# Down-projection of the last block: loads of weights and residual issued in turn with the activation blocks

## The chip, the cores and the metric

The kernel runs as one program on one core of a Trainium2 chip. The metric is device time in microseconds (us) of one execution. The time before is the median of three timed executions; one further execution was profiled, and every row shown here comes from that one.

## What is computed

The reference is a stack of two blocks on a sequence of 1024 tokens with 1024 features, in float32: a first block (attention with a pooled branch, then a gated convolution), and a second block (attention with a forgetting gate beside a short convolution, then a feed-forward part). The change lies in the very last part, the second half of the feed-forward part:

```python
hn = rms_norm_2(h, norm_mlp_g[layer])
a = jnp.square(jax.nn.relu(jnp.einsum('bld,df->blf', hn, w_ff1[layer])))
h = h + jnp.einsum('blf,fd->bld', a, w_ff2[layer])
h = rms_norm_2(h, final_norm_g)
```

The second product multiplies 1024 x 4096 activations by a 4096 x 1024 weight matrix, adds the residual and is followed by the final norm.

## The kernel before

**Precision and tiles.** Every float32 operand is split into a high and a low half of a shorter float type: `hi` (line 381) copies the high half on ScalarE (ACT), `lo` (line 384) takes the rest on VectorE (DVE). A product is then three matmuls (high by high, high by low, low by high), each 128 x 128 stationary by 128 x 512 moving.

**Seven steps instead of eight.** The product is done in the manner of Strassen and Winograd: the activations, the weights and the result are cut in two by two quarters, and seven products of quarters, the entries of `steps` (line 1720), replace eight. I number them 0 to 6 here. For a step the left operand is a stored combination of activation quarters (`11`, `s1`, `s2`, `s4`, `s3`, `12`, `22`), which the up-projection before (class `Up`, line 174) wrote to DRAM; the right operand is a combination of weight quarters, named `b11`, `t1`, `t2`, `b22`, `t3`, `b21`, `t4` after its function (lines 1678 to 1701).

**Inside a step** (loop at line 1733) the 2048 rows of the inner dimension are walked in eight blocks p of 256. Each block loads a tile `act` of 512 KB (line 1735, two buffers of the tag `wf`), splits it into `ah` and `al`, makes the right operand and splits it into `bh` and `bl` (three buffers each for the a and the b halves), and issues 24 matmuls: 4 banks of PSUM, 2 halves of 128 rows, 3 products. A step has 8 x 24 = 192 matmuls. After it, four additions on DVE (line 1763) put the banks onto the residual tile `res`.

**Where the right operands come from.** All of them call `weights` (line 1668), which loads a 512 KB tile of the weight matrix.
- Step 0 (`b11`) loads the eight tiles `x` and keeps them.
- Step 1 (`t1`) loads eight tiles `w` and subtracts `x` from them, into `x`, on DVE (line 1675).
- Step 2 (`t2`) loads eight tiles `y`, keeps them and forms `x` minus `y`. Step 3 (`b22`) uses `y` and loads no weights.
- Steps 4, 5 and 6 (`t3`, `b21`, `t4`) load eight tiles `w` each. Tiles `w` have two buffers (the tag `wh`).

**The residual** is loaded in four quarters of four DMAs of 256 KB (lines 1740 to 1743). They are written in the code behind block 3 of steps 0, 1, 2 and 4, ahead of the addition that needs them.

**What sets the order of the work.** The code is only traced in the order it is written. When the program is built, a scheduler that simulates the kernel in time gives each engine its own list of instructions: of those ready, each engine takes the one that is ready first, so an instruction that waits for nothing can come far ahead of its place in the code. The lists are fixed from then on: an engine runs its list in order, and an instruction that waits holds up all behind it. All loads of this part are in the list of SyncE's queue (SP), and those of the up-projection, its stores among them, too. Waiting for a buffer is such a wait: `act` of block p + 2 can be issued when `al` of block p has been made, because that was the last reader of the buffer.

Of the kernel before, what the change touches and what calls it, by code (L numbers as in the profile page):

```python
# [39 lines left out]
HALF = slice(0, 512), slice(512, 1024)  # L40
# [291 lines left out]
class Kernel:  # L332
# [1318 lines left out]
    def feed_down(self, one):  # L1651


        nc, a = self.nc, self.a
        hold = self.pool("d1", "right", 3)
        left = self.pool("d2", "left", 3)
        xp = self.psum_pool("pxdown", "pd")
        res_pool = self.pool("res3", "right")
        res = res_pool[1].tile([128, NT, D], F32, name="res")
        gfin = one.tile([128, D], F32, tag="last", name="gfin")  # L1660
        nc.sync.dma_start(out=gfin, in_=a["fing"].partition_broadcast(128))
        kept = {}

        def tile(name, p):
            pool = hold if p < 2 and name == "x" else left
            return pool[1].tile([128, 2, 512], F32, tag=f"{name}{p}", name=f"{name}{p}", bufs=1)

        def weights(j, l, p, t=None):
            t = t or self.stream.tile([128, 2, 512], F32, tag="wh", name="w2")
            r0 = 2048 * j + 256 * p  # L1670
            nc.sync.dma_start(out=t, in_=a["ff2"][r0:r0 + 256, HALF[l]].rearrange("(k p) c -> p k c", p=128))
            return t

        def minus(out, x, y):
            nc.vector.tensor_tensor(out=out, in0=x, in1=y, op=ALU.subtract)
            return out

        def b11(p):
            kept["x", p] = weights(0, 0, p, tile("x", p))
            return kept["x", p]  # L1680

        def t1(p):
            x = kept["x", p]
            return minus(x, weights(0, 1, p), x)

        def t2(p):
            kept["y", p] = weights(1, 1, p, tile("y", p))
            return minus(kept["x", p], kept["y", p], kept["x", p])

        def b22(p):  # L1690
            return kept["y", p]

        def t3(p):
            t = weights(0, 1, p)
            return minus(t, kept["y", p], t)

        def b21(p):
            return weights(1, 0, p)

        def t4(p):  # L1700
            return minus(kept["x", p], weights(1, 0, p), kept["x", p])

        def split(pool, tag, src):
            h, l = (pool[1].tile([128, 2, 512], F32R, tag=tag + x, name=tag + x) for x in "hl")
            self.hi(h, src)
            self.lo(l, src, h)
            return h, l

        def matmuls(bank, i, k, left, right, first, last, fresh):
            (ah, al), (bh, bl) = left, right  # L1710
            c = slice(i * 128, i * 128 + 128)
            for j, (st, mv) in enumerate(((ah, bh), (ah, bl), (al, bh))):
                nc.tensor.matmul(  # L1713
                    out=bank, lhsT=st[:, k, c], rhs=mv[:, k, :], start=(fresh and first and j == 0),
                    stop=(last and j == 2), skip_group_check=not fresh,
                )

        odd = None
        even = None
        steps = (  # L1720
            ("11", b11, 0, 0), ("s1", t1, 4, 1), ("s2", t2, 0, 1), ("s4", b22, 0, 1),
            ("s3", t3, 4, 1), ("12", b21, 0, 0), ("22", t4, 4, 0),
        )
        quarters = {0: (0, 0), 1: (4, 1), 2: (0, 1), 4: (4, 0)}
        for n, (name, right, t0, h) in enumerate(steps):
            fresh = n in (0, 1, 5)
            if n == 0:
                even = [self.bank("pd", 4) for _ in range(4)]
            elif fresh:
                odd = [self.pj(), self.pj(), self.ps(), self.ps()]  # L1730
            banks = odd if n % 2 else even
            ops = []
            for p in range(8):
                t = self.stream.tile([128, 2, 512], F32, tag="wf", name="act")
                nc.sync.dma_start(out=t, in_=self.act[name, p])
                ops.append((split(left, "a", t), split(hold, "b", right(p))))
                end = n == 6 and p >= 6
                if end and p == 6:
                    continue
                if p == 3 and n in quarters:  # L1740
                    r0, c = quarters[n]
                    for i in range(r0, r0 + 4):
                        nc.sync.dma_start(out=res[:, i, HALF[c]], in_=self.x3[i * 128:(i + 1) * 128, HALF[c]])
                if not end:
                    for k in range(2):
                        for i in range(4):
                            matmuls(banks[i], i, k, *ops[p], p + k == 0, p == 7 and k == 1, fresh)
            squares = {}
            if n == 6:
                for i in range(4):  # L1750
                    ms = squares[i] = self.tiny(2, "fms")
                    junk = left[1].tile([128, 512], F32, tag="r", name="junk")
                    self.half_square(ms, 1, res[:, t0 + i, HALF[1]], junk)
                    nc.gpsimd.tensor_scalar(
                        out=ms[:, 1:2], in0=ms[:, 1:2], scalar1=EPS_B, scalar2=None, op0=ALU.add
                    )
            for i in range(4):
                if n == 6:
                    for p in (6, 7):
                        for k in range(2):  # L1760
                            matmuls(banks[i], i, k, *ops[p], False, p == 7 and k == 1, fresh)
                x = res[:, t0 + i, HALF[h]]
                nc.vector.tensor_tensor(out=x, in0=x, in1=banks[i], op=ALU.add)
                if n > 4:
                    self.final_norm(t0 + i, [res[:, t0 + i, z] for z in HALF], gfin, left[1], squares.get(i))
        self.close(res_pool, hold, left, xp)
# [94 lines left out]
```

## Time and profile before

| | before |
|---|---|
| median of 3 runs | 1979.45 us (1978.23 to 1982.49) |
| profiled execution | 1975.94 us |
| span in its profile | 1974.2 us |
| TensorE (PE) busy | 1906.5 us, 97% |
| VectorE (DVE) busy | 1340.4 us, 68% |
| ScalarE (ACT) busy | 906.0 us, 46% |
| GpSimd (POOL) busy | 542.5 us, 27% |
| data moved by DMA | 212.15 MB, 107 GB/s on average |

The span is the time from the first to the last instruction in the profile; the profiled execution's own time is 1.7 us longer. Busy shares are means over the whole kernel; the part that the change touches is the stretch from about 1640 us to the end. A row of a timeline gives start, duration, engine, line, operation, output and inputs, and in brackets how long the engine had been idle before it and what ended that wait. A row with "x2" stands for two instructions in a row.

### The profile page before, as it was taken

The page shows a single profiled execution, that of the slowest core. Times are in us where ns is not written, and L with a number is a line of the kernel's source. Part 1 is how long each engine was busy: PE and PEld are TensorE (multiplying, and loading weights), DVE is VectorE, ACT ScalarE, POOL GpSimd, SP SyncE. Part 2 cuts the span into 40 slices and gives each one's busy share as a digit, 9 for nine tenths or more (in the row PEclk, how much of TensorE's full clock was granted, in tenths as well). Part 3 has the DMA queues.
Part 4 walks back from the last instruction along what each step waited for, and adds up shares of the span by engine and source line. Part 5 has one row for each costly group of instructions (what it writes and reads, how often), then busy time and mean ns, then how long its engine had stood idle before and what let it go on. Part 6 is the DMA issues. An engine that isn't in the chain of part 4 may idle for free. (4 is left out here: it accounts for less than half of the span.)

```text
span 1974.2 us, 25561 instructions
## 1 busy us (share of the span) xinstructions
PE 1906.5 (97%) x9584; PEld 1616.1 (82%) x9584; DVE 1340.4 (68%) x2045; ACT 906.0 (46%) x1577; POOL 542.5 (27%) x433
## 2 busy tenths in 40 slices
PE   7999999899999899999999999999999998999998
PEld 5888788687778678898999998887888886788886
DVE  7788656699898665565656655657776766754666
ACT  5556234456664665555444544324333323333333
POOL 4022602479997221001010101202433320000003
PEclk9999999999999999999999999999999999999999
DMA  4110143111122732111111202523534448622564
GB/s 151 51 47 26 67 135 117 40 54 52 36 79 85 236 107 73 45 44 44 48 49 44 76 27 99 192 98 102 171 133 166 149 160 321 228 96 96 192 214 149
DMA packets 122747, 212.15 MB, mean 107 GB/s; under 512 B 9576, under 2 KB 59112, under 8 KB 122624
## 3 DMA queue, kind: packets, MB, share of 16 engines
q1 hardware_dynamic: 120320, 206.34, 30.9%
q10 hardware_dynamic: 2304, 4.20, 0.6%
q8 instruction: 75, 1.23, 0.3%
q14 instruction: 48, 0.39, 0.1%
HBM read 156.46 MB, written 54.03 MB: 107 GB/s over the span
## 5 line engine op out<-in xcount | busy, mean ns | idle before, releaser
L1155 POOL TENSOR_TENSOR side<-side,tap 128x1024 f32<-128x1024 f32 (+1 forms) x99 | 235.6, 2386 | 24.9 <-ACT tap L1154 17.8
L1161 DVE SCALAR_TENSOR_TENSOR acc<-glu,dw,acc 128x1024 f32<-128x1024 f32 (+1 forms) x162 | 193.8, 1238 | 11.5 <-ACT acc L1159 10.2
L425 PE MATMUL pj<-c0h,wl 128*128 128x512 f32 (+1 forms) x496 | 187.8, 379 | 5.7 <-DVE wl L386 5.7
L425 PE MATMUL pj<-c0h,wh 128*128 128x512 f32 (+1 forms) x496 | 188.9, 381 | 4.3 <-ACT gt L1192 2.7
L425 PE MATMUL pj<-c0l,wh 128*128 128x512 f32 (+1 forms) x496 | 187.4, 378 | 0.0
L425 PE MATMUL pj<-c1h,wh 128*128 128x512 f32 (+1 forms) x496 | 176.3, 356 | 3.6 <-ACT sg L1129 1.8
L425 PE MATMUL pj<-c1l,wh 128*128 128x512 f32 (+1 forms) x496 | 177.0, 357 | 0.0
L425 PE MATMUL pj<-c1h,wl 128*128 128x512 f32 (+1 forms) x496 | 176.6, 356 | 0.0
L1154 ACT ACTIVATE tap<-glu,dw 128x1024 f32<-128x1024 f32 (+1 forms) x99 | 103.8, 1055 | 78.9 <-POOL side L1155 78.4
L386 DVE TENSOR_TENSOR al<-act,ah 128x1024 fp32r<-128x1024 f32 x56 | 68.3, 1223 | 91.5 <-ACT ah L382 91.3
L382 ACT ACTIVATE ah<-act 128x1024 fp32r<-128x1024 f32 x56 | 59.3, 1060 | 154.5 <-PE ps L1713 75.4
L382 ACT ACTIVATE ph<-pt 128x512 fp32r<-128x512 f32 (+3 forms) x144 | 72.8, 516 | 104.7 <-PE pt L1461 68.1
L1713 PE MATMUL pd<-bh,ah 128*128 128x512 f32 x256 | 100.2, 397 | 12.1 <-ACT ah L382 12.1
L386 DVE TENSOR_TENSOR pl<-pt,ph 128x512 fp32r<-128x512 f32 (+3 forms) x144 | 83.3, 586 | 41.0 <-ACT ph L382 40.6
L425 PEld LDWEIGHTS pj<-c0h,wl 128*128 128x128 f32 x496 | 94.0, 190 | 19.0 <-DVE wl L386 6.1
L425 PEld LDWEIGHTS pj<-c0h,wh 128*128 128x128 f32 x496 | 94.1, 190 | 18.4 <-ACT gt L1192 3.1
L425 PEld LDWEIGHTS pj<-c1h,wh 128*128 128x128 f32 x496 | 94.1, 190 | 18.0 <-ACT sg L1129 2.3
L386 DVE TENSOR_TENSOR wl<-wf,wh 128x1024 fp32r<-128x1024 f32 (+1 forms) x66 | 90.6, 1373 | 23.5 <-ACT wh L382 23.2
L425 PEld LDWEIGHTS pj<-c1l,wh 128*128 128x128 f32 x496 | 94.2, 190 | 13.0 <-DVE c1l L386 0.4
L425 PEld LDWEIGHTS pj<-c1h,wl 128*128 128x128 f32 x496 | 94.4, 190 | 12.4
L425 PEld LDWEIGHTS pj<-c0l,wh 128*128 128x128 f32 x496 | 93.8, 189 | 12.6 <-issue 0.2
L1713 PE MATMUL pd<-bl,ah 128*128 128x512 f32 x256 | 101.2, 395 | 0.0
(607 smaller groups left out, 5105.1 us busy)
## 6 DMA issues: line engine op xcount, KB each, us to landing
wf<-in_w SPq DMA_DIRECT2D x63, 512.0 KB, 3.5
raw<-in_ff SPq DMA_DIRECT2D x32, 512.0 KB, 4.8
w<-in_ff SPq DMA_DIRECT2D x32, 512.0 KB, 4.3
act<-acts SPq DMA_DIRECT2D x32, 512.0 KB, 3.2
acts<-s SPq DMA_DIRECT2D x48, 256.0 KB, 3.8
act<-act SPq DMA_DIRECT2D x24, 512.0 KB, 3.9
wf<-in_wo SPq DMA_DIRECT2D x20, 512.0 KB, 3.5
cb<-cum SPq DMA_DIRECT2D x8, 520.0 KB, 3.7
```

The lines of the kernel that those rows point to most:

```text
L382: self.nc.scalar.activation(out=out, in_=src, func=AF.Copy, scale=scale)
L386: return self.nc.vector.tensor_tensor(out=out, in0=src, in1=hi.bitcast(F32), op=ALU.subtract)
L425: self.nc.tensor.matmul(out=p[:m, :n], lhsT=st[:, k, :], rhs=mv[:, k, :], start=(k == 0 and j == 0), stop=(k == KD - 1 and j == 2),)
L1154: nc.scalar.activation(out=tap, in_=src, func=AF.Copy, scale=w)
L1155: nc.gpsimd.tensor_tensor(out=side, in0=side, in1=tap, op=ALU.add)
L1161: nc.vector.scalar_tensor_tensor(out=acc, in0=src, scalar=w, in1=acc, op0=ALU.mult, op1=ALU.add)
L1713: nc.tensor.matmul(out=bank, lhsT=st[:, k, c], rhs=mv[:, k, :], start=(fresh and first and j == 0), stop=(last and j == 2), skip_group_che ...
```

## The change

`feed_down` keeps a list `turn` of the issued loads of activation blocks. Each load of weights, and each load of a residual quarter, is traced inside `issue_after` with the latest of them. That adds an edge to the scheduler's graph: on SP's list, this load stands somewhere behind that load of `act`. It is an edge of issue order alone: nothing waits at run time for the `act` load to land. No instruction is added, removed or resized.

```diff
-        kept = {}
+        kept, turn = {}, []
...
         def weights(j, l, p, t=None):
             t = t or self.stream.tile([128, 2, 512], F32, tag="wh", name="w2")
             r0 = 2048 * j + 256 * p
-            nc.sync.dma_start(out=t, in_=a["ff2"][r0:r0 + 256, HALF[l]].rearrange("(k p) c -> p k c", p=128))
+            src = a["ff2"][r0:r0 + 256, HALF[l]].rearrange("(k p) c -> p k c", p=128)
+            with self.tc.issue_after(turn[-1].ins):
+                nc.sync.dma_start(out=t, in_=src)
             return t
...
                 t = self.stream.tile([128, 2, 512], F32, tag="wf", name="act")
-                nc.sync.dma_start(out=t, in_=self.act[name, p])
+                turn.append(nc.sync.dma_start(out=t, in_=self.act[name, p]))
                 ops.append((split(left, "a", t), split(hold, "b", right(p))))
...
                     for i in range(r0, r0 + 4):
-                        nc.sync.dma_start(out=res[:, i, HALF[c]], in_=self.x3[i * 128:(i + 1) * 128, HALF[c]])
+                        with self.tc.issue_after(turn[-1].ins):
+                            nc.sync.dma_start(out=res[:, i, HALF[c]], in_=self.x3[i * 128:(i + 1) * 128, HALF[c]])
```

## Rows read from the trace of the kernel before

**Rows 1.** Windows: busy us (and instructions) per engine, then PE clock, DMA share, GB/s.

```profile
1650.00:1675.00 25.00, 21.11 (x91) 16.73 (x89) 13.20 (x13) 6.68 (x7) 0.00 (x0) 0.99 1.05 405
1675.00:1700.00 25.00, 19.81 (x77) 15.55 (x78) 15.37 (x14) 7.42 (x7) 0.00 (x0) 0.93 0.94 352
1700.00:1725.00 25.00, 25.00 (x112) 20.69 (x111) 21.73 (x21) 10.05 (x10) 0.00 (x0) 1.00 0.39 141
...
1850.00:1875.00 25.00, 25.00 (x112) 20.70 (x111) 13.35 (x12) 10.05 (x10) 0.00 (x0) 1.00 0.63 201
```

**Rows 2.** Timeline of PE, single rows between 1643 and 1879 us.

```profile
1643.28 0.39 PE L236 MATMUL pd<-t4h,a22l 128*128 128x512 f32 x1
1647.14 0.73 PE L1713 MATMUL pd<-bh,ah 128*128 128x512 f32 x1 [3.48 <-ACT ah L382]
...
1650.66 1.09 PE L1713 MATMUL pd<-bh,al 128*128 128x512 f32 x4
...
1662.03 0.50 PE L1713 MATMUL pd<-bh,ah 128*128 128x512 f32 x1 [2.09 <-ACT ah L382]
...
1677.09 0.50 PE L1713 MATMUL pd<-bh,ah 128*128 128x512 f32 x1 [3.89 <-ACT ah L382]
...
1692.58 0.50 PE L1713 MATMUL pd<-bh,ah 128*128 128x512 f32 x1 [2.68 <-ACT ah L382]
...
1704.33 0.39 PE L1713 MATMUL pj<-bh,ah 128*128 128x512 f32 x1
...
1747.85 0.39 PE L1713 MATMUL pd<-bh,ah 128*128 128x512 f32 x1
...
1834.89 0.39 PE L1713 MATMUL pd<-bh,ah 128*128 128x512 f32 x1
...
1878.41 0.39 PE L1713 MATMUL pj<-bh,ah 128*128 128x512 f32 x1
```

**Rows 3.** Timeline of ACT, single rows of step 0.

```profile
1644.60 1.06 ACT L382 ACTIVATE bh<-x 128x1024 fp32r<-128x1024 f32 x1 [8.46 <-DMA x<-in_ff]
...
1659.97 1.06 ACT L382 ACTIVATE bh<-x 128x1024 fp32r<-128x1024 f32 x1 [4.38 <-PE pd L1713]
1660.93 1.04 ACT L382 ACTIVATE ah<-act 128x1024 fp32r<-128x1024 f32 x1
...
1675.98 1.06 ACT L382 ACTIVATE ah<-act 128x1024 fp32r<-128x1024 f32 x1 [1.69 <-DMA act<-act]
```

**Rows 4.** Timeline of SP's queue, single rows of step 0.

```profile
1649.03 0.41 SPq L1671 DMA_DIRECT2D y<-in_ff  x1
1649.96 0.35 SPq L1735 DMA_DIRECT2D act<-act  x1
...
1668.44 14.45 SPq L1743 DMA_DIRECT2D res<-x3s  x16
```

**Rows 5.** DMA issues, 1600 to 1720 us: count, KB each, median us to landing.

```profile
w<-in_ff SPq DMA_DIRECT2D x10, 512.0 KB, 5.3
...
y<-in_ff SPq DMA_DIRECT2D x8, 512.0 KB, 10.0
res<-x3s SPq DMA_DIRECT2D x16, 256.0 KB, 5.3
act<-act SPq DMA_DIRECT2D x7, 512.0 KB, 10.0
```

**Rows 6.** DMA issues, 1830 to 1910 us, the same columns.

```profile
w<-in_ff SPq DMA_DIRECT2D x15, 512.0 KB, 4.3
act<-act SPq DMA_DIRECT2D x10, 512.0 KB, 3.2
```

**Rows 7.** Timeline of DVE, the first two low halves of step 0.

```profile
1648.09 2.35 DVE L386 TENSOR_TENSOR al<-act,ah 128x1024 fp32r<-128x1024 f32 x2
```

**Rows 8.** Timelines of SP and DVE, the last loads and low half of step 6.

```profile
1927.97 0.37 SPq L1671 DMA_DIRECT2D w<-in_ff  x1
...
1942.90 0.33 SPq L1735 DMA_DIRECT2D act<-act  x1
...
1951.34 1.22 DVE L386 TENSOR_TENSOR bl<-x,bh 128x1024 fp32r<-128x1024 f32 x1
```

## The prediction, made before the changed kernel ran

> **What bounds the kernel now.** I read the table of windows first. From 1700 us on PE works without a break at the full clock, 112 matmuls in 25 us; in the two windows before it is busy for 21.11 and 19.81 us of 25, with the DMA engines at a share of 1.05 and 0.94 and 405 and 352 GB/s [rows 1]. So PE bounds the down-projection nearly everywhere, and only its beginning loses time, where the DMA engines are full.
>
> The timeline of PE gives the size. The starts of steps 0, 1, 2, 4 and 5 are at 1647.14, 1704.33, 1747.85, 1834.89 and 1878.41 [rows 2]. Steps 1 and 4 take 43.52 us each, which for 192 matmuls is 0.2267 us a matmul and 5.44 us a block; steps 2 and 3 together take 87.04, the same. Step 0 has as many matmuls and takes 57.19: 13.67 us too many. Three idles make 2.09 + 3.89 + 2.68 = 8.66 of them, all ended by `ah` on ACT [rows 2]. The first eight matmuls, 1647.14 to 1650.66, take 3.52 where 8 x 0.2267 is 1.81, so 1.71 us go to the lower of the clock's two levels (1.2 against 2.4 GHz) after the idle of 3.48 us that opens the step. The other 3.3 us are matmuls slowed after the later idles and short waits.
>
> The timeline of ACT says why `ah` is late. Before the first idle ACT stands at `bh` of block 4 until PE has done block 1, and `ah` of block 2 is behind it in ACT's list; before the second, `ah` waits for its load [rows 3]. Both come from loads that land late: `act` of block 2 is issued at 1649.96 behind a load of `y`, and 16 residual issues hold SP for 14.45 us [rows 4]. In this stretch `act` takes a median of 10.0 us to land, and `y` 10.0; in steps 4 and 5 `act` takes 3.2 and `w` 4.3 [rows 5, 6]. None of the `y` and only one residual quarter of four is needed in step 0. That is 8 x 0.52 + 12 x 0.26 = 7.3 MB, 18 us of transfer at 405 GB/s, in front of or among blocks that PE waits for.
>
> **The change part by part.** It removes no instruction. The 48 weight loads and 16 residual loads get an edge; what moves is their place in SP's list, with what that does to the scheduler's lists for ACT and DVE.
>
> *Loads of `x` in step 0.* `x` of blocks 0 and 1 must follow `act` of those blocks, which are in by then, so the opening idle stays and with it the 1.71 us of slow start. From block 2 on, `x` follows `act`, which needs the first `al` made: the pair of `al` starts at 1648.09 and takes 2.35 [rows 7], so about 1649.3. `act` and `x` of block 2 are then issued at about 1650. With 0.4 us to issue and 4.3 to land (a weight load in steps 4 and 5 [rows 6]), then `bh` for 1.06 and `bl` for the 1.2 of a low half [rows 3, 7], the block is ready at 1657. PE wants it at 1647.14 + 1.71 + 2 x 5.44 = 1659.7, so there are 2.7 us to spare. If the load took the 10.0 us of the crowded stretch [rows 5], it would be ready at 1662.7, a wait of 3.0. I take no wait, since only four loads of half a megabyte stand in the queue then; 0 and 3.0 are the ends.
>
> *Loads of `y`, of `w` of step 1 and of the later residual quarters* leave step 0. What is left there is 1.05 MB a block, 193 GB/s at 5.44 us, and with one residual quarter 9.4 MB in 43.5 us, 217 GB/s, far below 405. Steps 4 and 5 run at such a load: 201 GB/s in a window of step 4, with PE full [rows 1]. The gain is the excess without its slow start, 13.67 - 1.71 = 11.96 us. Its lower end is 11.96 - 3.0, less one more spell of slow clock of 1.7, about 7.3.
>
> *Steps 1 and 2* lose their prefetch: `w` and `y` now land in their own step, and up to 16 subtractions of 1.2 us on DVE, part of which ran in step 0, move there. Per block DVE has a subtraction and two low halves, 3 x 1.2 = 3.6 us of 5.44. Step 4 has the same form, weights loaded block by block and subtracted, and takes 43.52, so I cost this at nothing. Its cover is the lead of a block: `act` of block p is issued once `al` of p - 2 is made, which is about 2.5 us after PE ends p - 5 (an `ah` and an `al`). With 4.3 to land, 0.4 to issue and 1.2 to subtract, the right operand is there 8.4 us after that end, and its buffers come free 10.9 after it, at the end of p - 3. The ends are 0 and, were the cover gone, what step 0 shows, 12 us a step.
>
> *The residual quarters* come 4 blocks, some 22 us, before their addition and land in 5.3 [rows 5]. *SP* issues as many loads as before; 64 of 0.4 us are 26 us spread over 305. The last stores of the up-projection stand in the same list; fewer loads come ahead of them than now.
>
> *Step 6* loses the most lead: its last `w` is issued at 1927.97, 15 us before the last `act` at 1942.90 [rows 8]. Behind it, it lands at about 1947.6; the subtraction, `bh` and `bl` bring 1951.1. The last `bl` now starts at 1951.34, and PE wants block 7 at 1878.41 + 43.52 + 6 x 5.44 + 6 x 0.23 = 1955.9. That is 0 us; with a landing of 10.0, about 1 us.
>
> **Sum.** -12.0 us. On the profiled execution's own time, 1975.94 (span 1974.2 and 1.7 around it), that is 1964; that execution lies 3.5 us below the median of the runs, and I take the difference off the median: 1979.45 - 12.0 = 1967.5. With 1 to 2 us for the median of a few runs (those of before spread over 4), 1965.5 to 1970 is this case's own range.
>
> **Rivals.** *Some of the stall stays.* The block 2 load is late by up to 3.0 us and the clock falls once more, or the scheduler leaves one `bh` ahead of an `ah` that PE needs sooner, as in rows 3. Two idles of that size would leave about 4 to 8 us: 1971 to 1976. For it speaks that the start of step 0 has little lead; against it, that steps 1 to 5 keep their order without a stall.
>
> *The opening gets better too.* The first `bh` waits for `x` 8.46 us, with `ah` behind it on ACT [rows 3]. A new list could bring `ah` first or `x` sooner. At most the idle of 3.48 and its 1.71 go: 1962. Against it: `x` of block 0 isn't held by anything that moves.
>
> *It changes nothing.* The edges bind only issue order; if the scheduler, which works with its own times, keeps ACT's list with `bh` in front of `ah`, the idles stay whatever the loads do: 1979. Against it: in all later steps, where `act` isn't crowded, the list has no such place that stalls PE.
>
> *The stalls move to steps 1 and 2.* Those two steps run without a break behind a prefetch that the change ends. If a weight load lands later than 6.8 us after its issue (the 2.5 us that the cover above has over, and 4.3), the subtraction comes after the buffers are free, `bh` holds up the next `ah` on ACT, and the next `act` is issued later still: step 0's chain. Two steps that lose 12.0 each, less the 12.0 saved, end at 1979.45 + 12 = 1991.5. For it: `w` and `y` took 5.3 and 10.0 us in the crowded stretch. Against it: 4.3 in steps 4 and 5, where nothing is loaded ahead by a step. The Trainium skill speaks for this rival: its page "DMA: Bandwidth & Descriptors", section "Rules for kernel authors", says to issue a DMA early and to wait on it late, and the change does the reverse. By that rule steps 1 and 2 would lose; the trace so far disagrees for step 0, where the early loads are what delays the needed ones.
>
> **How the numbers follow.** The forecast has 0.62, stalls that stay in part 0.14, a better opening 0.07, no effect 0.06, stalls in steps 1 and 2 0.11. Forecast, part and opening hold 0.83 and span 1962 to 1976, which is the range. A measurement of this kernel can tell about 0.2%, 4 us, from no change. Faster than 1975.5 come the forecast, the opening and nearly all of the partial case: 0.82; same 0.07; slower 0.11.
>
> **What would show it.** In the timeline of PE, step 0 should last about 45.3 us in place of 57.19, with no idle over 1 us behind the opening one, and steps 1 and 2 still 43.52. SP's list should alternate `act` and weights from block 2 on, with four residual loads together behind block 3 of steps 0, 1, 2 and 4, and the DMA rate in 1650 to 1690 should fall to about 220 GB/s, with `act` landing in under 5 us. I would be wrong if step 0 still showed idles ended by `ah`, if an idle appeared in step 1, 2 or 6, or if the part before 1643 moved.

## The result, and the profile after

| | before | after |
|---|---|---|
| median, 5 runs each on the same chip | 1979.45 us (1978.23 to 1982.49) | 1962.92 us (1961.58 to 1966.35) |
| ratio, with its 95% interval | | 0.9919 [0.9905, 0.9932] |
| profiled execution | 1975.94 us | 1961.58 us |
| span in its profile | 1974.2 us | 1959.8 us |
| PE busy | 1906.5 us | 1902.9 us |

The change makes the kernel faster by 16.5 us of the medians; 1967.5 was forecast, and 1962 to 1976 was the range. The two profiled executions differ by 14.4 us, and from here on I ask where these come from.

The table of windows of the changed kernel (columns as in [rows 1]):

```profile
1650.00:1675.00 25.00, 25.00 (x112) 20.68 (x111) 12.38 (x11) 11.72 (x12) 0.00 (x0) 1.00 0.91 326
1675.00:1700.00 25.00, 25.00 (x112) 20.73 (x111) 17.89 (x18) 8.65 (x9) 0.00 (x0) 1.00 0.65 228
1700.00:1725.00 25.00, 25.00 (x112) 20.72 (x111) 16.96 (x16) 10.05 (x10) 0.00 (x0) 1.00 0.55 194
```

PE, which had 21.11 and 19.81 us in the first two of them, is busy for all 25, with 112 matmuls at the full clock. The DMA engines still come to a share of 0.91 at first, but no longer to 1.05, and 405 and 352 GB/s have become 326 and 228.

The timeline of PE, single rows:

```profile
1640.94 0.39 PE L236 MATMUL pd<-t4h,a22l 128*128 128x512 f32 x1
1644.69 0.50 PE L1715 MATMUL pd<-bh,ah 128*128 128x512 f32 x1 [3.36 <-ACT ah L382]
...
1689.96 0.39 PE L1715 MATMUL pj<-bh,ah 128*128 128x512 f32 x1
...
1733.48 0.39 PE L1715 MATMUL pd<-bh,ah 128*128 128x512 f32 x1
...
1820.52 0.39 PE L1715 MATMUL pd<-bh,ah 128*128 128x512 f32 x1
...
1864.04 0.39 PE L1715 MATMUL pj<-bh,ah 128*128 128x512 f32 x1
```

These answer to [rows 2]. Step 0 lasts from 1644.69 to 1689.96, which is 45.27 us in place of 57.19. The three idles that `ah` ended are gone; the one that opens the step is there with 3.36. Steps 1 and 4 take 43.52 as before, and so do the others. The last matmul starts 8.95 us before the end of the span, 8.94 before the change. So 11.92 of the 14.4 us come from step 0. The other 2.4 come from ahead of it: the last matmul of the up-projection starts at 1640.94 in place of 1643.28. The two are taken apart below.

The lists that PE follows, in two timelines of the changed kernel. First ACT, blocks 0, 2 and 3 of step 0:

```profile
1642.15 1.06 ACT L382 ACTIVATE bh<-x 128x1024 fp32r<-128x1024 f32 x1 [8.35 <-DMA x<-in_ff]
...
1649.95 1.06 ACT L382 ACTIVATE ah<-act 128x1024 fp32r<-128x1024 f32 x1 [2.90 <-DMA act<-act]
1651.48 1.06 ACT L382 ACTIVATE bh<-x 128x1024 fp32r<-128x1024 f32 x1 [0.47 <-DMA x<-in_ff]
1653.77 1.06 ACT L382 ACTIVATE ah<-act 128x1024 fp32r<-128x1024 f32 x1 [1.23 <-DMA act<-act]
```

Then SP's queue:

```profile
1645.92 0.32 SPq L1737 DMA_DIRECT2D act<-act  x1
1646.33 0.39 SPq L1673 DMA_DIRECT2D x<-in_ff  x1
...
1652.30 0.32 SPq L1737 DMA_DIRECT2D act<-act  x1
1652.71 0.39 SPq L1673 DMA_DIRECT2D x<-in_ff  x1
1655.79 1.74 SPq L1746 DMA_DIRECT2D res<-x3s  x4
```

On ACT `ah` and `bh` now alternate, where before the `bh` of block 4 stood ahead of the `ah` of block 2 [rows 3]. On SP `act` and `x` alternate, and the residual takes four issues in 1.74 us where sixteen took 14.45 [rows 4]. The DMA issues from 1600 to 1720 us of the changed kernel say what that does to the landing (count, KB each, median us to landing):

```profile
x<-in_ff SPq DMA_DIRECT2D x8, 512.0 KB, 5.4
w<-in_ff SPq DMA_DIRECT2D x8, 512.0 KB, 4.8
act<-act SPq DMA_DIRECT2D x7, 512.0 KB, 4.0
res<-x3s SPq DMA_DIRECT2D x8, 256.0 KB, 5.3
y<-in_ff SPq DMA_DIRECT2D x2, 512.0 KB, 4.4
```

`act` lands in 4.0 us where it took 10.0 [rows 5], and two loads of `y` stand in this stretch where eight stood.

### The profile page after: what moved, and what is told of

It reads as the page before. It is cut to its first block, busy times and chain, and to the rows that moved or that the text cites. A ratio compares the mean times of both kernels' runs of the same rounds, so it can differ in the third digit from the quotient of the medians.

```text
span 1959.8 us, 25557 instructions
## 1 busy us (share of the span) xinstructions
PE 1902.9 (97%) x9584; PEld 1615.4 (82%) x9584; DVE 1340.1 (68%) x2045; ACT 905.8 (46%) x1577; POOL 538.3 (27%) x433
## 3 DMA queue, kind: packets, MB, share of 16 engines
q8 instruction: 75, 1.23, 0.3%
```

## The experiments

Kernels that were timed side by side on one chip are shown with the same median of before. A ratio is to that median.

### The two kernels once more: what belongs to the change

Both kernels unchanged, the changed one twice.

> The kernel before, unchanged. Of the 16.5 us between the medians my working explains 12.0, all in step 0. Theory A: the rest is not the change but executions that differ in how many spells of low clock they have, about 1.7 us each; then this run is within 0.1% of the kernel before, its step 0 in the profile is 57.2 us give or take one spell (55.5 to 59.0), and stretches ahead of 1640 us differ from the first profile by such spells. Rival B: the kernel before loses the rest in step 0 too, because its three idles drop the clock more often than the first profile showed; then step 0 lasts 59 to 62 us here.

> The changed kernel, unchanged. Theory A: step 0 lasts 45.3 us again (43.6 if the clock does not fall at its opening), no idle of PE behind the opening one, steps 1 to 6 at 43.52, and the gain on the same chip lies between 12 and 15 us once the clock spells even out (ratio 0.9924 to 0.9940). Rival B: the gain stays at 16 us or more (ratio below 0.992).

> The changed kernel a third time: the first comparison gave a ratio of 0.9919 (0.9905 to 0.9932), the second 0.9940 (0.9927 to 0.9952). If the gain is step 0 alone, 12 us, 0.9939 is the mean to expect and this one lies between 0.9930 and 0.9950. If there is a further steady gain of 4 us, it lies under 0.9930.

| | median | before beside it | ratio | step 0 | last matmul of the up-projection starts |
|---|---|---|---|---|---|
| before again | 1978.75 (12 runs) | 1978.20 | 0.9998 [0.9989, 1.0008] | 59.63 | 1642.61 |
| after again | 1966.47 (6 runs) | 1978.20 | 0.9940 [0.9927, 0.9952] | 45.30 | 1645.45 |
| after, third time | 1963.73 (5 runs) | 1978.72 | 0.9925 [0.9912, 0.9937] | 45.25 | 1641.90 |

The part ahead of step 0 shows no effect of the change. The same code of after starts the last matmul of the up-projection at 1640.94, 1645.45 and 1641.90, that of before at 1643.28 and 1642.61: means of 1642.8 and 1642.9. In the first two profiles the difference can be seen in the window from 40 to 50 us, far ahead of the change. Before:

```profile
40.00:50.00 10.00, 10.00 (x43) 8.17 (x43) 8.30 (x11) 3.39 (x7) 4.61 (x4) 0.85 0.16 53
```

After:

```profile
40.00:50.00 10.00, 10.00 (x50) 8.36 (x49) 8.29 (x12) 2.95 (x6) 4.18 (x4) 1.00 0.16 53
```

PE is busy for the whole of it in both, but 43 matmuls stand against 50, at a granted clock of 0.85 against 1.00: a piece of the stretch ran at the lower level in one execution and not in the other.

Step 0 of before is not one number either. The second profile of before, timeline of PE:

```profile
1646.51 0.50 PE L1713 MATMUL pd<-bh,ah 128*128 128x512 f32 x1 [3.51 <-ACT ah L382]
...
1661.40 0.50 PE L1713 MATMUL pd<-bh,ah 128*128 128x512 f32 x1 [2.09 <-ACT ah L382]
...
1676.21 0.50 PE L1713 MATMUL pd<-bh,ah 128*128 128x512 f32 x1 [3.64 <-ACT ah L382]
...
1692.37 0.79 PE L1713 MATMUL pd<-bh,ah 128*128 128x512 f32 x1 [4.98 <-ACT ah L382]
```

The first idle is the same 2.09, but the last is 4.98 where the first profile has 2.68 [rows 2], and step 0 takes 59.63. That is the time that rival B expected (59 to 62), not that of theory A (55.5 to 59.0), though longer idles make most of it (10.71 us in place of 8.66) and not the clock that B named. The third ratio of after, 0.9925, lies just outside the 0.9930 to 0.9950 that was named for a gain of 12 us. The two profiles of before, 57.19 and 59.63, have a mean of 58.4 against 45.27, 45.30 and 45.25 of the changed kernel: 13.1 us, not 11.9. Over all runs of unchanged code, from four comparisons, the mean of before is 1978.55 (69 runs, 1973.66 to 1982.83) and that of after 1964.57 (16 runs, 1961.58 to 1968.82): 14.0 us. Step 0 explains 13.1 of them; 0.9 us is left over, which two profiles of before can't settle.

### Parts of the change: which loads have to be held back

The gate is left on some loads only. Residual alone: `weights` loses its `with`. Weights alone: the residual loses it.

```diff
-            with self.tc.issue_after(turn[-1].ins):
-                nc.sync.dma_start(out=t, in_=src)
+            nc.sync.dma_start(out=t, in_=src)
```

> Only the residual loads are put behind their activation blocks; weights are free as before, so all y and six w still come in step 0, and three bh stand ahead of the ah of block 2. 'Late landing': 8 MB of y and w in place of 11.5 with the residual; the first two idles stay, the last shortens, step 0 lasts 52 to 57 us, gain 1 to 5 us (ratio 0.9975 to 0.9995). Rival 'the residual burst is the cause', since its 16 issues hold SP for 14 us in a row: step 0 falls under 50 us.

> All weight loads are put behind their activation blocks, the sixteen residual loads are free as before; on SP's list they stand in step 0 behind blocks 4, 5 and 6 of the activations, 4, 3 and 9 of them. 'Late landing' with the size of the overload as the cause: step 0 then moves 12.6 MB in 43.5 us, 290 GB/s, under the 405 that the engines reach, so the time is that of the changed kernel, step 0 at 45 to 46 us, ratio 0.993 to 0.995. Rival 'residual burst': 9 residual loads in a row ahead of a block delay it once, an idle of 1 to 4 us near block 7, step 0 47 to 50 us.

Step 0's `x` alone (residual free too), and everything but step 0's `x` with `> 8`:

```diff
-            with self.tc.issue_after(turn[-1].ins):
+            if len(turn) <= 8:
+                with self.tc.issue_after(turn[-1].ins):
+                    nc.sync.dma_start(out=t, in_=src)
+            else:
                 nc.sync.dma_start(out=t, in_=src)
```

> Only the eight weight loads of step 0 are put behind their activation block; weights of the later steps and the residual are free as before. On ACT's list the high halves then alternate (ah, bh) through step 0, while SP's list still has six y, one w and another y ahead of the third activation block. Theory 'late landing' (the step stalls because its blocks land behind loads that nobody needs yet): the stalls stay, activations land at 8 to 10 us, step 0 lasts 53 us or more. Rival 'list' (it stalls because bh stands ahead of ah on ACT): the stalls go, step 0 lasts 45 to 47 us, 1965 to 1969 us.

> All loads are put behind their activation block except the eight weight loads of step 0, which stand together ahead of the third activation block; on ACT's list three bh (blocks 2 to 4) stand ahead of the ah of block 2, as in the kernel before. Theory 'late landing': 3.1 MB more ahead of that block cost 8 us once, hidden for the most part by two blocks of work; step 0 lasts 45 to 49 us. Rival 'list': the ah of block 2 waits until PE has done block 1, an idle of about 2 us as before, and the others repeat; step 0 lasts 50 us or more.

| held back | median | before beside it | ratio | step 0 | idles of PE in step 0 behind the opening |
|---|---|---|---|---|---|
| nothing (before, two profiles) | | | | 57.19, 59.63 | three, 8.66 and 10.71 us |
| residual | 1975.27 (11 runs) | 1978.08 | 0.9981 [0.9970, 0.9993] | 52.51 | 2.12, 2.55 |
| `x` | 1971.31 (7 runs) | 1978.20 | 0.9968 [0.9956, 0.9980] | 52.53 | 4.19, 0.32 |
| all but `x` | 1967.03 (5 runs) | 1978.20 | 0.9944 [0.9931, 0.9957] | 47.70 | 2.09 |
| weights, `x` included | 1965.63 (5 runs) | 1978.72 | 0.9935 [0.9924, 0.9947] | 46.27 | none |
| all (after, beside `x` and all but `x`) | 1966.47 (6 runs) | 1978.20 | 0.9940 [0.9927, 0.9952] | 45.30 | none |
| all (after, beside weights) | 1963.73 (5 runs) | 1978.72 | 0.9925 [0.9912, 0.9937] | 45.25 | none |

With `x` alone held back, `y`, `w` and the residual come early as before. SP's queue in that kernel:

```profile
1645.05 3.44 SPq L1676 DMA_DIRECT2D y<-in_ff  x5
...
1649.85 0.75 SPq L1740 DMA_DIRECT2D act<-act  x1
```

and ACT:

```profile
1661.07 1.06 ACT L382 ACTIVATE ah<-act 128x1024 fp32r<-128x1024 f32 x1 [11.57 <-DMA act<-act]
1663.00 1.06 ACT L382 ACTIVATE bh<-x 128x1024 fp32r<-128x1024 f32 x1 [0.88 <-DMA x<-in_ff]
```

Eight loads that only steps 1 and 2 need go out ahead of the `act` of block 2: five of `y` in the first row, one `y` ahead of it, a `w` and a `y` behind it. ACT's list has `ah` in front of `bh` here, and ACT then stands idle for 11.57 us, for that load alone. PE's idle of 4.19 us is behind that wait. So late landing costs time without any help from ACT's list. The 52.53 us are a little under the 53 or more that 'late landing' expected, and far from the 45 to 47 of 'list'.

With all but `x` held back, `act` lands in a median of 4.8 us from 1640 to 1690, and one idle is left. Blocks 2 and 3 still land late, since five `x` go out just ahead of them. SP's queue of that kernel, and the time to landing of the second of these loads (tile `act`, 1650.5 to 1651 us):

```profile
1648.95 0.38 SPq L1740 DMA_DIRECT2D act<-act  x1
...
1650.53 0.38 SPq L1740 DMA_DIRECT2D act<-act  x1
```

```profile
DMA to landing us min/median/max: 9.6/9.6/9.6
```

ACT, then PE, of that kernel:

```profile
1660.54 1.06 ACT L382 ACTIVATE bh<-x 128x1024 fp32r<-128x1024 f32 x1 [4.38 <-PE pd L1718]
1661.50 1.99 ACT L382 ACTIVATE ah<-act 128x1024 fp32r<-128x1024 f32 x2
```

```profile
1662.59 0.50 PE L1718 MATMUL pd<-bh,ah 128*128 128x512 f32 x1 [2.09 <-ACT ah L382]
```

This is the first idle of before to the hundredth, with the same 4.38 us in which ACT waits at a `bh` for PE [rows 2, 3]. Here it isn't ended by a landing: the later of the two `act` was in at 1650.53 + 9.6 = 1660.1, ahead of that `bh`, and both `ah` run behind it without a wait. In before the two causes nearly coincide at this place. Its `act` of block 2, issued at 1649.96 [rows 4], took (tile `act`, 1649.9 to 1650.3 us):

```profile
DMA to landing us min/median/max: 10.2/10.2/10.2
```

It was in at 1660.2, and the `bh` in front held its `ah` only 0.8 us longer, to 1660.93 [rows 3].

So step 0 had two causes. The edge on `x` puts `ah` and `bh` in turn on ACT; step 0 is 47.70 - 45.27 = 2.4 us shorter with it. This is read from one profile without that edge, and the times don't confirm it: on one chip the medians are 1967.03 without and 1966.47 with it, and the intervals of the ratios overlap. The edges on what later steps need make up the rest: 9.5 to 11.9 us, from 57.19 or 59.63 to 47.70, and 11.2 us of the medians. So far 'late landing' expected the 47.70 rightly (45 to 49), and 'list' the idle of 2 us, but not its repeats. The parts don't add up from the other side: `x` alone held back takes 4.7 to 7.1 us off step 0, though the list's share above is 2.4. Its loads, held back, also leave the queue to others; how much of the 4.7 to 7.1 is which wasn't measured.

The residual's burst hurts only on top of the early weights. Holding it back alone leaves step 0 at 52.51 and brings 2.8 us of the median, less than the 4.7 to 7.1 that this one profile shows in step 0. (That execution was the slowest of its 11, 1979.60 us, since its step 0 starts only at 1655.45, 8.3 us later than in before.) Leaving it free behind the held weights costs nothing that can be seen: the sixteen residual loads go out between 1659 and 1675 us, and no idle appears. The 1.0 us by which step 0 is longer there (46.27) stands behind its opening, an idle of 3.98 and a longer piece at the lower clock; the intervals of the two ratios overlap.

### ACT's list alone

The kernel before with one thing added: on ACT each `bh` follows its block's `ah`. No load gets an edge.

```diff
+        highs = []
...
-            self.hi(h, src)
+            if tag == "a":
+                highs.append(nc.scalar.activation(out=h, in_=src, func=AF.Copy, scale=1.0))
+            else:
+                with self.tc.issue_after(highs[-1].ins):
+                    nc.scalar.activation(out=h, in_=src, func=AF.Copy, scale=1.0)
```

> No load is tied to an activation block; instead, on ACT alone, each bh is put behind the ah of its block, so that the list alternates through step 0 as in the changed kernel. SP's list has four more x ahead of the third activation block, and y, w and residual quarters among the next ones. 'Late landing': activations still land at 7 to 10 us or later, step 0 lasts 52 us or more, at most 5 us are gained (ratio 0.9975 to 1.001). 'List': step 0 falls to 48 us or less (ratio under 0.9955).

Measured: 1977.29 us (11 runs) beside 1978.08, a ratio of 0.9996 [0.9988, 1.0005], and a step 0 of 59.78. The timeline of PE:

```profile
1678.00 2.08 PE L1719 MATMUL pd<-bh,ah 128*128 128x512 f32 x4 [7.15 <-ACT bh L1711]
...
1693.39 1.19 PE L1719 MATMUL pd<-bh,ah 128*128 128x512 f32 x4 [2.75 <-ACT bh L1711]
```

and of ACT:

```profile
1662.47 1.06 ACT L1708 ACTIVATE ah<-act 128x1024 fp32r<-128x1024 f32 x1 [4.40 <-DMA act<-act]
...
1675.94 1.06 ACT L1708 ACTIVATE ah<-act 128x1024 fp32r<-128x1024 f32 x1 [11.47 <-DMA act<-act]
```

The idle of 2.09 is gone, and the next one has grown to 7.15, as `ah` waits 11.47 us for its load. The scheduler also put SP's list in a somewhat different order: `act` of block 2 goes out at 1647.88, ahead of every `y`, where before had it at 1649.96 behind one [rows 4], so the end of the first idle isn't the list's alone. In this run a list in the right order gains nothing that can be seen while the later loads land late; the 2.4 us above were read with the loads of later steps held back.

### Everything one block later: how much lead is needed

After, with the code issuing `act` one block ahead, so that each weight load stands behind the `act` of the *next* block, 5.44 us of PE's work later.

```diff
+        tiles = []
+
+        def load_act(m):
+            t = self.stream.tile([128, 2, 512], F32, tag="wf", name="act")
+            turn.append(nc.sync.dma_start(out=t, in_=self.act[steps[m // 8][0], m % 8]))
+            tiles.append(t)
...
-                t = self.stream.tile([128, 2, 512], F32, tag="wf", name="act")
-                turn.append(nc.sync.dma_start(out=t, in_=self.act[name, p]))
+                while len(tiles) < min(8 * n + p + 2, 56):
+                    load_act(len(tiles))
+                t = tiles[8 * n + p]
```

> The changed kernel with every weight load put behind the activation block after its own, one block of 5.44 us later. The cover worked out in the prediction leaves 2.5 us; if the weights' lead is that short, each block of steps 1, 2, 4, 5 and 6 loses up to 3 us, and the kernel is slower than before (over 1990 us). Rival: PE itself wants bh and bl some 5 us later than ACT could take them, the buffers hide the lag, and only block 1 of step 0, whose weights now wait for the first al, loses 1 to 4 us: 1966 to 1971 us, steps 1 to 6 at 43.52.

Measured: 1970.54 us (7 runs) beside 1978.08, 0.9968 [0.9956, 0.9980]. Steps 1 to 5 still take 43.52 us each. Their loads go out later, but early enough: the first `w` of step 1 is issued at 1685.39, 13.6 us ahead of the step's first matmul at 1699.03, where after has 1670.88 and 1689.96, 19.1 us. What is lost lies at the two ends, by the timeline of PE:

```profile
1659.18 1.59 PE L1715 MATMUL pd<-bh,ah 128*128 128x512 f32 x4 [2.35 <-ACT bh L382]
...
1941.76 0.50 PE L1715 MATMUL pd<-bl,ah 128*128 128x512 f32 x1 [1.52 <-DVE bl L386]
```

Block 1 of step 0 waits for its `x` (step 0 takes 49.51, 4.2 us more than in after), and one block of step 6 for a `bl` behind the subtraction of a late `w` (2.6 us more). So the rival of the expectation held but for step 6, and the prediction's rival of stalls in steps 1 and 2 has at least a whole block of room before it would begin.

### The opening

First, after with each `bh` behind its `ah` on ACT, by the edit shown above. Then the same, with `x` of block 0 loaded as the first of all by one extra load of 512 KB into a buffer that the up-projection uses (its kept copy follows in its turn), and with the halves of block 0's activations in such buffers too.

```diff
-            h, l = (pool[1].tile([128, 2, 512], F32R, tag=tag + x, name=tag + x) for x in "hl")
+            if tag == "a" and not highs:
+                h, l = (self.stream.tile([128, 2, 512], F32R, tag="wl", name=tag + x) for x in "hl")
+            else:
+                h, l = (pool[1].tile([128, 2, 512], F32R, tag=tag + x, name=tag + x) for x in "hl")
...
+            first = weights(0, 0, p) if p == 0 else None
...
+            return first or kept["x", p]
```

> The changed kernel with each bh put behind its ah on ACT and nothing else; it tells how much of the opening idle of 3.4 us is ACT's order and how much the late first weight block. ACT then does the last relu of the up-projection (0.6), ah (1.06) and bh (1.06) behind the last matmul of the up-projection: an idle of 2.5 to 2.8 us, 0.6 to 0.9 less, and no difference to the changed kernel that a ratio could show (0.992 to 0.995). If the order were all of it, the idle would fall under 1 us.

> The changed kernel with the opening of step 0 prepared ahead: its first weight block is loaded once more into a stream buffer that is free some 30 us earlier (one more load of 512 KB; the kept copy follows), its ah and al stand in stream buffers too, and each bh is put behind its ah on ACT. If the opening idle of 3.4 us is the wait for that weight block and for ah behind bh, it falls under 1 us and the spell of low clock behind it (1.8 us) goes in most executions: step 0 lasts 43.5 to 44 us, 4 to 5 us less than the changed kernel, ratio to the kernel before 0.9905 to 0.9925. Rival: the idle stays because bh or the banks come free only at the end of the up-projection: the time of the changed kernel, ratio 0.993 to 0.995.

With ACT's list alone the opening idle falls from 3.36 to 2.58 and is then ended by `bh`. The timeline of ACT says what it consists of:

```profile
1642.07 0.60 ACT L281 ACTIVATE okh<-pd 128x512 f32<-128x512 f32 x1 [7.56 <-PE pd L236]
1642.56 1.05 ACT L1710 ACTIVATE ah<-act 128x1024 fp32r<-128x1024 f32 x1
1643.51 1.05 ACT L1713 ACTIVATE bh<-x 128x1024 fp32r<-128x1024 f32 x1
```

`okh` is the last work of the up-projection and waits for its last matmul on PE; `ah` and `bh` follow it without a wait. These three in a row are the idle, so `x` isn't what PE waits for in this list. It wouldn't allow a much earlier start either: in after, the first `bh` waits for `x` until 1642.15, 0.8 us behind the end of that last matmul at 1641.33. Step 0 stays at 45.25, and the median is 1963.95 (5 runs) beside 1978.72, 0.9927 [0.9916, 0.9939], which can't be told from after. With the early `x` and the buffers the timeline of PE is:

```profile
1642.24 0.39 PE L236 MATMUL pd<-t4h,a22l 128*128 128x512 f32 x1
1642.47 0.39 PE L1725 MATMUL pd<-bh,ah 128*128 128x512 f32 x1
...
1686.01 0.39 PE L1725 MATMUL pj<-bh,ah 128*128 128x512 f32 x1
```

PE goes from the up-projection to step 0 without an idle and without a fall of the clock, and step 0 takes 43.54. The median is 1959.99 us (5 runs, 1957.57 to 1965.26) beside 1978.08, 0.9911 [0.9896, 0.9926], the lowest median here, though its interval overlaps with those of after. It wasn't timed beside after on one chip; the means, 1960.8 of its 5 runs and 1964.6 of after's 16, are 3.8 us apart, where the idle of 3.36 and the slow start of 1.7 would make 5.1. The edit changes ACT's list, the load of `x` and the buffers of `ah` and `al` at once; of these only the list was run alone.

## Why the prediction was right

**Step 0 and the three idles.** Right, and nearly to the number: 45.3 was forecast and 45.27, 45.30 and 45.25 were measured, with no idle behind the opening one. The opening kept its idle (3.36, 3.33, 3.72) and its slow start (45.27 - 43.52 = 1.75, forecast 1.71).

**The reason given.** Right on both counts, with unequal weights. The prediction named `bh` ahead of `ah` on ACT and late landing, and said that both come from loads that land late. The runs separate them by step 0 of their profiles: holding back what later steps need is worth 9.5 to 11.9 us, and the place on ACT's list 2.4 in addition (in one profile; the times don't confirm it), but nothing by itself. It isn't quite a consequence of the landing, as the prediction had it: with the loads of later steps held back and `x` free, the `bh` still stands in front and the idle of 2.09 stays, although the `act` are in. It also weighs less in the first idle of before, where the prediction named it: there the `act` was in only 0.8 us ahead of its `ah`.

**Block 2 in time.** Right. Its `act` and `x` were issued at 1645.92 and 1646.33, and its `bh` starts at 1651.48, so that with a `bl` of 1.23 behind it the block is ready at about 1653.8. PE wants it at 1644.69 + 1.75 + 2 x 5.44 = 1657.3. That is 3.5 us to spare, forecast 2.7.

**The size.** The forecast of -12.0 us was small. The mis-sized term is the excess of step 0 before, 13.67 us, taken as if every execution had it. The second profile has 59.63 - 43.52 = 16.11; 10.71 - 8.66 = 2.05 us of the difference are longer idles. A stall that hangs on how crowded transfers land varies, and one profile is one draw of it. The mean of the two gives 13.1 of the 14.0 us between all runs. The remainder of the 16.5 us of the first comparison is its own draw: the repeats gave ratios of 0.9940 and 0.9925. That its 1962.92 lies inside 1962 to 1976 is in part luck. The working's own range was 1965.5 to 1970, and the lower end of 1962 came from the rival of a better opening, which didn't happen.

**Steps 1 and 2, and their cover.** The cost of nothing was right, the cover was mis-sized. The prediction put it at 2.5 us over a landing of 4.3; a delay of a whole block, 5.44 us, cost these steps nothing. The chain there was reckoned to the moment at which ACT could take the operands, whereas PE wants them only when the blocks made ahead are used up: the first `w` of step 1 goes out 19.1 us ahead of its use in the changed kernel, and 13.6 us were still enough. So the 11 in 100 for the rival that ends at 1991.5 was generous. The prediction read that rival's rule, to issue a DMA early and wait on it late (the Trainium skill, "DMA: Bandwidth & Descriptors", section "Rules for kernel authors"), as a loss in steps 1 and 2. These runs disagree with that reading: step 0, which got the early loads of others, lost 9.5 to 11.9 us by them, and steps 1 and 2, whose loads came later, lost none.

**The residual, SP and step 6.** Nothing, as costed: four residual issues take 1.74 us, and step 6 shows no idle. The timeline of SP's queue has its last loads:

```profile
1927.75 0.33 SPq L1737 DMA_DIRECT2D act<-act  x1
1928.13 0.49 SPq L1673 DMA_DIRECT2D w<-in_ff  x1
```

They go out 20.2 and 20.6 us into the step, which starts at 1907.56; before, that `act` went out 1942.90 - 1921.93 = 21.0 us into it, and the last `w` 6.0 us [rows 8]. By the timeline of DVE the last `bl` still starts as long after the start of the step as before, 29.4 us:

```profile
1936.97 1.22 DVE L386 TENSOR_TENSOR bl<-x,bh 128x1024 fp32r<-128x1024 f32 x1
```

So the lost lead of `w`, 14.5 us, was lead that nothing used.

**The DMA rate.** Wrong, without consequence: about 220 GB/s was forecast for 1650 to 1690. The window has 273:

```profile
1650.00:1690.00 40.00, 40.00 (x178) 33.11 (x178) 23.44 (x21) 16.37 (x17) 0.00 (x0) 1.00 0.77 273
```

The bytes of step 0 were spread evenly over it in the working. In fact blocks 2 to 5 go out as fast as buffers come free, four pairs between 1645.92 and 1658.05, so the rate is high first (326 from 1650 to 1675) and 228 after; and the first loads of step 1, from 1670.88 on, fall into the window too. `act` still landed under the 5 us that were named.

**"If the part before 1643 moved".** It moved, by 2.3 us, and the prediction had called that a sign against itself. The sign was badly chosen: executions of the same code spread over 4.5 us there.

## What to carry to other kernels

A load that has its buffer free isn't free of cost: issued early, it stands in the queue ahead of a load that is needed now, and shares the engines with it; here `act` took 10.0 us to land in place of 4.0. Look for stretches where the DMA engines are full while PE has idles, list which of the bytes moving there the present stage needs, and hold the rest back until the stage that uses them is near: here the first load of step 1 went out 19.1 us ahead of the step, and 13.6 us was still enough. A stall that hangs on crowded transfers should be read from two or three profiles before its size is put into a sum.

## What was unexpected of the hardware

An idle of PE of a given length does or doesn't cost clock. Windows behind the three later idles of before again (2.09, 3.64 and 4.98 us; columns as in [rows 1]):

```profile
1660.00:1666.00 6.00, 4.60 (x20) 3.84 (x21) 3.59 (x3) 2.40 (x3) 0.00 (x0) 1.00 1.05 411
1676.00:1682.00 6.00, 5.79 (x25) 4.80 (x26) 2.58 (x3) 1.24 (x3) 0.00 (x0) 1.00 1.05 402
1692.00:1698.00 6.00, 5.63 (x13) 4.46 (x14) 5.97 (x6) 1.37 (x2) 0.00 (x0) 0.50 0.79 257
```

The granted clock stays at 1.00, the level of 2.4 GHz, behind the first two and is 0.50, 1.2 GHz, behind the third, where 13 matmuls stand in place of 25. But it isn't the length alone: in other profiles it fell behind 2.12 (residual alone), 2.35 (one block later), 2.58 (`ah` first) and 3.89 us (before), and did not behind 2.55 (residual alone) and 2.68 us (before). Where it fell, it cost some 1.7 us as at the opening, behind the 4.98 about twice that (16.11 - 10.71 - 1.7 = 3.7). In a sum an idle of 2 to 4 us therefore has two prices, some 1.7 us apart.

Executions of one program also differ by more than several of the parts measured here: before by 9.2 us over 69 runs on several chips, after by 7.2 over 16. In the one window laid side by side above, from 40 to 50 us, the difference was the granted clock under the same instructions.
